# Three gated merges computed by rows instead of by columns, with the sum turned on TensorE

## The chip, the cores and the metric

One Trainium2 chip, one of its cores. The metric is the time of one execution in device microseconds; the time quoted for a kernel is the median of its runs. All arithmetic is 32-bit; matrix operands are split into a high and a low part (`hi`, `lo`, type float32r), so that each product is made of three matmuls: high by high, high by low, low by high.

## What is computed

One block of a streaming encoder on 256 rows of width 2048. Three attention branches (memory, DSA, stick-breaking) each leave 1024 channels per row. The part that the change touches is the merge:

```
gates  = sigmoid(gl + b_gate)                # gl = h @ w_in[:, GL:GL+6144], three blocks of 2048
merged = gates[0] * (o_sb  @ w_branch[0])
       + gates[1] * (o_dsa @ w_branch[1])
       + gates[2] * (o_mem @ w_branch[2])
x = x + merged @ w_out                       # the output projection
```

After it come a norm, an up projection to 11008 columns, a short causal convolution, a gate, and a down projection.

## The kernel before, in words

**Weights.** All weights lie in DRAM as tiles of 128 partitions by up to 1024 values, in the order of use. `w_tiles` (L148) fetches the next one on SP's queue into `raw` (4 buffers), ScalarE copies it to `whi` and VectorE subtracts to get `wlo` (3 buffers each, at high priority), and then the matmuls of that tile follow. A tile of a matrix with 512 columns to a chunk holds 2 row blocks of 128; with 256 columns, 4 row blocks.

**Two ways to multiply.** `proj_cols` (L178) makes the weights stationary: for each row block and each 128 weight columns it runs `whi` against the high and low parts of all 256 rows (512 moving columns) and `wlo` against the high parts (256 moving columns). The result stands with channels on partitions. `proj_rows` (L166) makes the activations stationary: for each row block and each of two row tiles of 128 it runs three matmuls with 512 weight columns moving. The result stands with rows on partitions. In a trace the first reads `pj<-xc,whi` and `pj<-xc,wlo`, the second `pj<-whi,xc` and `pj<-wlo,xc`; `xc` is the normalized input, and `om`, `od`, `osb` (branch outputs), `x2c`, `fc` and `mg` stand in its place elsewhere. A tile is 16 matmuls by columns (8 of 512 and 8 of 256 moving) and 12 by rows (all of 512): 6144 moving columns either way.

**The merge** (L522) runs three times: for the memory branch while the DSA attention is under way, for DSA while stick-breaking attention is under way, and for stick-breaking alone. Each has 8 chunks of 256 columns: 4 tiles of gate weights, an evacuation and tanh on `th`, 2 tiles of branch weights, an evacuation to `pbr`, and the product added into `acc`. The last merge also splits the sum into `mg`, the operand of the output projection. So each merge has 48 weight tiles.

**The order of other work.** After each weight tile, `step()` (L106) runs one due entry of `soon` or one piece of the generator at the head of `later` (attention heads). These pieces put a few matmuls (`s`, `o`) or transposes (`t`) between tiles. The scheduler then fixes each engine's order.

Of the kernel before, what the change touches and what calls it, by code (L numbers as in the profile page):

```python
# [11 lines left out]
F32 = mybir.dt.float32  # L12
# [7 lines left out]
P = 128  # L20
# [15 lines left out]
R1, R2 = -0.6368202810903829, 1.3473041101248473  # 2**12 and 2**22 modulo 2 pi  # L36
# [9 lines left out]
def weight_chunks():  # L46
    """The weight columns in the order of their use: (matrix, row blocks, first column, columns)."""
    for c in range(4):
        yield "kv", KD, c * 512, 512
    for base, n in ((QM, 1024), (KB, 1024), (QB, 1024), (VB, 512), (QI, 256), (QI + 256, 328), (VB + 512, 512)):  # L50
        for c in range(0, n, 512):
            yield "in", KD, base + c, min(512, n - c)
    for br in (2, 1, 0):
        for c in range(0, D, 256):
            yield "in", KD, GL + br * D + c, 256
            yield "b%d" % br, D // 2 // P, c, 256
        if br == 2:
            for base, n in ((KA, 256), (QA, 256), (VA, 512)):
                for c in range(0, 1024, n):
                    yield "in", KD, base + c, n  # L60
    for c in range(4):
        yield "out", KD, c * 512, 512
    for c in range(0, DFF, 256):
        for half in range(2):
            yield "up", KD, half * DFF + c, min(256, DFF - c)
    for c0, n in DOWN:
        yield "down", NFF, c0, n


def weight_tiles():  # L70
    """The chunks cut into tiles of up to 1024 values a partition: (matrix, first row block, row blocks, c0, n)."""
    first = True
    for name, nk, c0, n in weight_chunks():
        j = 0
        while j < nk:
            kn = 1 if first else min(8, 1024 // n, nk - j)
            yield name, j, kn, c0, n
            j += kn
            first = False
# [7 lines left out]
def hybrid_block(ctx: ExitStack, tc: tile.TileContext, x, xT, mem, memT, pos, inv, prm, gqk, wts, out):  # L87
# [14 lines left out]
    # Other work is spread between the weight tiles: each tile is followed by one due entry of `soon`, or else by one  # L102
    # step of the generator at the head of `later`.
# [26 lines left out]
    def heads(n, first, second, third):  # L130
        """The three stages of n heads, two heads under way at a time."""
        first(0)
        yield
        first(1)
        yield
        for h in range(n):
            yield
            second(h)
            yield
            yield  # L140
            if h + 2 < n:
                first(h + 2)
            yield
            third(h)
# [3 lines left out]
    def w_tiles(name, nk, c0, n):  # L148
        """The weight columns c0..c0+n by row block as pairs (hi, lo) of float32r tiles."""
        j = 0  # L150
        while j < nk:
            at, (name_, j_, kn, c0_, n_) = next(tiles)
            assert (name_, j_, c0_, n_) == (name, j, c0, n), (name, j, c0, n)
            raw = wraw.tile([P, 1024], F32, name="raw")
            nc.sync.dma_start(raw[:, :kn * n], wts[at, :, :kn * n])  # L155
            hi = whl.tile([P, 1024], F32R, name="whi")
            lo = whl.tile([P, 1024], F32R, name="wlo")
            with tc.high_priority():
                nc.scalar.activation(hi[:, :kn * n], raw[:, :kn * n], AF.Copy)  # L159
                nc.vector.tensor_sub(lo[:, :kn * n], raw[:, :kn * n], hi[:, :kn * n].bitcast(F32))  # L160
            for k in range(kn):
                yield j + k, hi[:, k * n:(k + 1) * n], lo[:, k * n:(k + 1) * n]
            step()
            j += kn

    def proj_rows(a, name, nk, c0, n):  # L166
        """A PSUM tile [128 rows, 2 row tiles, n] of a.T @ w[:, c0:c0+n]; a is [128, nk, (hi, lo), 256]."""
# [10 lines left out]
    def proj_cols(a, name, nk, c0, n):  # L178
        """A PSUM tile [128 columns, column blocks, (main, rest), 256 rows] of w[:, c0:c0+n].T @ a."""
# [8 lines left out]
    def split(dst, src, scale=1.0):  # L188
        """dst[:, .., (hi, lo), :] of scale * src."""
# [29 lines left out]
    hb = const.tile([P, 48], F32, name="hb")  # L219

    def load_constants():
# [4 lines left out]
        nc.vector.tensor_scalar_mul(hb, prm_sb[:, B_GATE:B_GATE + 48], 0.5)  # L226

    def rsqrt(pool, v, n):
        """1 / sqrt(v) of a small tile [128, n], by Newton's iteration."""
# [9 lines left out]
    def row_squares(ss, rows, src):  # L239
        """The sums of squares of the rows of src [256, 2048], one half of a row tile a step."""  # L240
# [8 lines left out]
    def row_rstd(pool, ss):  # L249
        """[128, 2] of 1 / rms over rows of 2048 with sums of squares ss."""  # L250
# [5 lines left out]
    def bcast_cols(pool, r, name):  # L256
        """[128, 256] with r's entry of row tile tt, row n in column tt * 128 + n of every partition."""
# [10 lines left out]
    with ExitStack() as actx:  # L268
# [54 lines left out]
        def heads256(ps, g0, dst, b0, wait, r=None, r2=None):  # L323
            """RMS norm over 256 channels of two heads in ps (row tiles tt), transposed to dst[:, b0.., rows]."""
# [72 lines left out]
        def weighted_values(o, pt, v_of):  # L397
            """o [128 channels, 256 rows] from pt: keys 0..127 by all rows, then keys 128..255 by rows 128..255."""
# [20 lines left out]
        # the angle modulo 2 pi: angle = 2**22 nh + 2**12 nl + rest, exact but for the last three steps  # L419
# [32 lines left out]
        def rope(dst, src, c1, s2, c2, s1, nh_, half):  # L452
            """dst = (x1 c1 - x2 s2, x2 c2 + x1 s1) for src [128, nh_, 2 * half] in PSUM."""
# [68 lines left out]
        # sigmoid(g) = (1 + tanh(g / 2)) / 2; the half is applied to the sum  # L522
        acc = []

        def merge(br, o, then=None):
            """Adds 2 * sigmoid(gate of branch br) * (o @ its projection) to acc; then(column blocks, sum) if given."""
            first = not acc
            if first:
                acc.extend(h8("acc").rearrange("p (b t) -> p b t", t=T) for _ in range(2))
            for c in range(8):  # L530
                pg = proj_cols(xc, "in", KD, GL + br * D + c * 256, 256)
                th = tg.tile([P, 2, T], F32, name="th")
                nc.scalar.activation(th, pg[:, :, 1, :], AF.Copy)
                nc.vector.tensor_add(th, pg[:, :, 0, :], th)
                for b in range(2):
                    i = br * 16 + c * 2 + b
                    nc.scalar.activation(th[:, b, :], th[:, b, :], AF.Tanh, scale=0.5, bias=hb[:, i:i + 1])
                pb = proj_cols(o, "b%d" % br, 8, c * 256, 256)
                a_ = acc[c // 4][:, (c % 4) * 2:(c % 4) * 2 + 2, :]
                t_ = tg.tile([P, 2, T], F32, name="pbr", bufs=2)  # L540
                nc.scalar.activation(t_, pb[:, :, 1, :], AF.Copy)
                nc.vector.tensor_add(t_, pb[:, :, 0, :], t_)
                if first:
                    nc.vector.scalar_tensor_tensor(a_, th, 1.0, t_, op0=ALU.add, op1=ALU.mult)
                    continue
                nc.vector.scalar_tensor_tensor(t_, th, 1.0, t_, op0=ALU.add, op1=ALU.mult)
                nc.vector.tensor_add(a_, a_, t_)
                if then is not None:
                    then(slice(2 * c, 2 * c + 2), a_)

# [64 lines left out]
        # columns 0..127: rows of tile 0 against keys 0..127; 128..383: rows of tile 1 against all keys  # L615
# [95 lines left out]
        # z is [key, row]: columns 0..255 keys of tile 0 by all rows, 256..383 keys of tile 1 by rows 128..255  # L711
# [37 lines left out]
        merge(0, osb, lambda blocks, a_: split(mg[:, blocks], a_, 0.5))  # L749

# [1 line left out]
        x2c = xp.tile([P, KD, 2, T], F32R, name="x2c", tag="xc")  # L752
        ss = const.tile([P, 2, 4], F32, name="ssx2")
        for c in range(4):
            ps = proj_rows(mg, "out", KD, c * 512, 512)
            x2 = []
            for tt in range(2):
                xr = tg.tile([P, 512], F32, name="xr", tag=("th", "pbr")[tt])
# [69 lines left out]
_ORDER = ["x", "xT", "mem", "memT", "pos", "inv", "prm", "gqk", "wts"]  # L828
# [38 lines left out]
```

## Time and profile before

| what | before |
|---|---|
| median of 3 runs | 1709.14 us (1707.66 to 1709.62) |
| span of the profiled execution | 1706.0 us, so 3.1 us less than the median |
| PE busy | 1695.3 us, 99% of the span |
| VectorE, ScalarE busy | 64%, 52% |
| TensorE clock granted | full in all 40 slices |
| the three merges | 321.91 to 475.03, 609.09 to 759.80, 759.80 to 895.48 us |

Busy time of PE adds pipelined matmuls, so 99% says that it nearly always had one in the pipe, not that it ran at its peak. What counts below is the distance from the start of one matmul to the start of the next. A few per cent of matmul records are missing, so distances are read between rows that stand on either side of a full group.

### The profile page before, as it was taken

How to read it: one execution, taken by the hardware profiler on the slowest of the kernel's cores; microseconds unless marked ns; L12 is line 12 of the kernel's file. 1: busy time of each engine (PE TensorE's matmuls, PEld its weight loads, DVE VectorE, ACT ScalarE, POOL GpSimd, SP SyncE). 2: the span in 40 equal slices, each digit the busy share in tenths (PEclk: the TensorE clock that was granted, in tenths of full speed). 3: DMA queues.
4: the chain of work that ended last, by engine and by line, in shares of the span. 5: the costliest groups of instructions: out<-in, count | busy, mean ns of one | idle time of the engine just before them, and what ended most of it. 6: DMA issues, size and time to landing. Idle time of an engine off the chain costs nothing.

```text
span 1706.0 us, 24002 instructions
## 1 busy us (share of the span) xinstructions
PE 1695.3 (99%) x9202; PEld 1466.1 (86%) x9202; DVE 1088.6 (64%) x1626; ACT 894.8 (52%) x1231; POOL 6.9 (0%) x58
## 2 busy tenths in 40 slices
PE   8999999999999999999999999999999999999999
PEld 6888889888888888888888888888888888888899
DVE  6686865786554455655655577777777777644443
ACT  7555554455544477645554555555555555433432
POOL 0000000000000000000000000000000000000000
PEclk9999999999999999999999999999999999999999
DMA  9755445544455554455556665555555555565663
GB/s 340 263 184 186 148 161 175 185 172 162 162 184 185 190 177 158 166 182 188 186 191 228 223 209 187 194 188 189 193 186 193 190 188 192 188 213 197 219 207 128
DMA packets 96516, 326.60 MB, mean 191 GB/s; under 512 B 10768, under 2 KB 16272, under 8 KB 96400
## 3 DMA queue, kind: packets, MB, share of 16 engines
q1 hardware_dynamic: 95536, 324.00, 55.3%
q8 instruction: 72, 1.18, 0.3%
q10 hardware_dynamic: 864, 1.06, 0.2%
q14 instruction: 44, 0.36, 0.1%
HBM read 320.82 MB, written 4.19 MB: 191 GB/s over the span
## 4 chain that ended last, share of the span: by engine, by line
PE 99%; DMA 0%; DVE 0%; ACT 0%; issue 0%; SPq 0%; DVEq 0%
PE pj L100 95%; PE s L100 2%; PE o L100 1%; DMA mf<-in_memT 0%; PE t L559 0%; PE t L771 0%; PE t L328 0%; PE t L681 0%; DVE xf L372 0%; ACT whi L159 0%; DVE wlo L160 0%; PE t L505 0%; ACT mc L190 0%; DVE xc L192 0%; SPq L155 0%
## 5 line engine op out<-in xcount | busy, mean ns | idle before, releaser
L160 DVE TENSOR_TENSOR wlo<-raw,whi 128x1024 fp32r<-128x1024 f32 (+2 forms) x591 | 719.7, 1218 | 569.7 <-ACT whi L159 568.4
L159 ACT ACTIVATE whi<-raw 128x1024 fp32r<-128x1024 f32 (+2 forms) x591 | 623.0, 1054 | 753.3 <-PE pj L100 579.1
L100 PE MATMUL pj<-x2c,whi 128*128 128x512 f32 x1376 | 477.5, 391 | 0.0
L100 PE MATMUL pj<-x2c,wlo 128*128 128x256 f32 x1376 | 385.5, 280 | 0.0
L100 PE MATMUL pj<-xc,whi 128*128 128x512 f32 x1024 | 366.9, 401 | 0.0
L100 PEld LDWEIGHTS pj<-x2c,whi 128*128 128x128 f32 x1376 | 257.3, 187 | 56.4
L100 PE MATMUL pj<-xc,wlo 128*128 128x256 f32 x1024 | 287.0, 280 | 0.0
L100 PEld LDWEIGHTS pj<-x2c,wlo 128*128 128x128 f32 x1376 | 260.1, 189 | 0.0
L100 PE MATMUL pj<-whi,xc 128*128 128x512 f32 (+2 forms) x768 | 231.7, 379 | 0.5 <-DVE xc L192 0.5
L100 PEld LDWEIGHTS pj<-xc,whi 128*128 128x128 f32 x1024 | 192.4, 188 | 45.6
L100 PE MATMUL pj<-whi,fc 128*128 128x512 f32 (+1 forms) x860 | 221.0, 347 | 0.0
L100 PEld LDWEIGHTS pj<-xc,wlo 128*128 128x128 f32 x1024 | 193.4, 189 | 0.3
L100 PEld LDWEIGHTS pj<-whi,fc 128*128 128x128 f32 x860 | 150.6, 189 | 20.1
L100 PEld LDWEIGHTS pj<-whi,xc 128*128 128x128 f32 x768 | 141.0, 188 | 25.5 <-DVE xc L192 1.0
L100 PE MATMUL pj<-wlo,fc 128*128 128x512 f32 (+1 forms) x430 | 149.1, 347 | 0.0
L100 PE MATMUL pj<-wlo,xc 128*128 128x512 f32 (+2 forms) x384 | 143.6, 374 | 0.0
L100 PEld LDWEIGHTS pj<-wlo,fc 128*128 128x128 f32 x430 | 81.4, 189 | 10.1
L100 PE MATMUL pj<-whi,mc 128*128 128x512 f32 x256 | 81.5, 397 | 5.6 <-ACT whi L159 5.6
L100 PEld LDWEIGHTS pj<-wlo,xc 128*128 128x128 f32 x384 | 72.3, 188 | 11.8
L100 PE MATMUL pj<-whi,mg 128*128 128x512 f32 x256 | 80.6, 392 | 0.0
L100 PEld LDWEIGHTS pj<-whi,mc 128*128 128x128 f32 x256 | 48.7, 190 | 16.0 <-ACT whi L159 6.1
L100 PEld LDWEIGHTS pj<-whi,mg 128*128 128x128 f32 x256 | 48.1, 188 | 9.9
(225 smaller groups left out, 1429.3 us busy)
## 6 DMA issues: line engine op xcount, KB each, us to landing
raw<-in_wts SPq DMA_DIRECT2D x578, 512.0 KB, 3.3
raw<-in_wts SPq DMA_DIRECT2D x5, 492.0 KB, 3.2
nat_rows<-in_mem SPq DMA_DIRECT2D x4, 512.0 KB, 6.5
nat_rows<-in_x SPq DMA_DIRECT2D x4, 512.0 KB, 6.5
xf<-in_xT SPq DMA_DIRECT2D x4, 512.0 KB, 5.6
xr<-in_x SPq DMA_DIRECT2D x8, 256.0 KB, 3.6
x2d<-xr SPq DMA_DIRECT2D x8, 256.0 KB, 4.2
mf<-in_memT SPq DMA_DIRECT2D x3, 512.0 KB, 8.1
```

Source lines behind the costliest of these rows:

```text
L100: nc.tensor.matmul(o, l, r, start=start, stop=stop, skip_group_check=True)
L159: nc.scalar.activation(hi[:, :kn * n], raw[:, :kn * n], AF.Copy)
L160: nc.vector.tensor_sub(lo[:, :kn * n], raw[:, :kn * n], hi[:, :kn * n].bitcast(F32))
```

## The change

The merge uses `proj_rows` with chunks of 512 columns, 4 to a merge (8 gate tiles and 4 branch tiles each, still 48 tiles and the same bytes of weights). The gate bias no longer comes with the tanh instruction as a value per partition; it is fetched from DRAM, the same 512 values to all 128 partitions, once for each row tile, into `th` before the gate result is added. `acc` stands by rows, so in the last merge each finished 512 columns are turned by 8 transposes (4 for each row tile) into a PSUM tile `t`, and split from there into `mg`. They are queued 3 and 4 steps after the end of the chunk.

```diff
-        for c in range(0, D, 256):
-            yield "in", KD, GL + br * D + c, 256
-            yield "b%d" % br, D // 2 // P, c, 256
+        for c in range(0, D, 512):
+            yield "in", KD, GL + br * D + c, 512
+            yield "b%d" % br, D // 2 // P, c, 512
...
-            for c in range(8):
-                pg = proj_cols(xc, "in", KD, GL + br * D + c * 256, 256)
-                th = tg.tile([P, 2, T], F32, name="th")
-                nc.scalar.activation(th, pg[:, :, 1, :], AF.Copy)
-                nc.vector.tensor_add(th, pg[:, :, 0, :], th)
-                for b in range(2):
-                    i = br * 16 + c * 2 + b
-                    nc.scalar.activation(th[:, b, :], th[:, b, :], AF.Tanh, scale=0.5, bias=hb[:, i:i + 1])
-                pb = proj_cols(o, "b%d" % br, 8, c * 256, 256)
-                a_ = acc[c // 4][:, (c % 4) * 2:(c % 4) * 2 + 2, :]
-                t_ = tg.tile([P, 2, T], F32, name="pbr", bufs=2)
-                nc.scalar.activation(t_, pb[:, :, 1, :], AF.Copy)
-                nc.vector.tensor_add(t_, pb[:, :, 0, :], t_)
...
+            for c in range(4):
+                cols = slice(c * 512, (c + 1) * 512)
+                th = tg.tile([P, 2, 512], F32, name="th")
+                for tt in range(2):
+                    nc.sync.dma_start(th[:, tt], bcast_rows(bg[:, br * D + c * 512:br * D + (c + 1) * 512], 512))
+                pg = proj_rows(xc, "in", KD, GL + br * D + c * 512, 512)
+                nc.vector.tensor_add(th, pg, th)
+                nc.scalar.activation(th, th, AF.Tanh, scale=0.5)
+                pb = proj_rows(o, "b%d" % br, 8, c * 512, 512)
+                for tt in range(2):
+                    a_ = acc[tt][:, cols]
+                    if first:
+                        nc.vector.scalar_tensor_tensor(a_, th[:, tt], 1.0, pb[:, tt], op0=ALU.add, op1=ALU.mult)
+                        continue
+                    nc.vector.scalar_tensor_tensor(th[:, tt], th[:, tt], 1.0, pb[:, tt], op0=ALU.add, op1=ALU.mult)
+                    nc.vector.tensor_add(a_, a_, th[:, tt])
                 if then is not None:
-                    then(slice(2 * c, 2 * c + 2), a_)
+                    then(c)
...
-        merge(0, osb, lambda blocks, a_: split(mg[:, blocks], a_, 0.5))
+        def turn_merged(c, tt):
+            pt = pa.tile([P, 512], F32, name="t")
+            for b in range(4):
+                at = (4 * c + b) * P
+                nc.tensor.transpose(pt[:, b * P:(b + 1) * P], acc[tt][:, at:at + P], ident)
+            split(mg[:, 4 * c:4 * c + 4, :, tt * P:(tt + 1) * P], pt.rearrange("p (b t) -> p b t", t=P), 0.5)
+        merge(0, osb, lambda c: [after(3 + tt, partial(turn_merged, c, tt)) for tt in range(2)])
```

In the output projection the two row tiles of the residual, `xr` before, become halves of one tile `xrow`.

On TensorE's queue, the third gate tile of the last merge's second chunk ends, and what follows, before the change at the same weights and after it. Before, columns run on without a break:

```order
L100 MATMUL pj<-xc,whi 128x512
L100 MATMUL pj<-xc,wlo 128x256
L100 MATMUL pj<-xc,whi 128x512
L100 MATMUL pj<-xc,wlo 128x256
L100 MATMUL pj<-xc,whi 128x512
```

After the change the same place reads (`t<-ident,acc` are the new transposes):

```order
L100 MATMUL pj<-whi,xc 128x512
L749 MATMUL t<-ident,acc 128x128 x4
L100 MATMUL pj<-whi,xc 128x512
L100 MATMUL pj<-wlo,xc 128x512
L100 MATMUL pj<-whi,xc 128x512 x2
L100 MATMUL pj<-wlo,xc 128x512
L100 MATMUL pj<-whi,xc 128x512 x2
L100 MATMUL pj<-wlo,xc 128x512
L100 MATMUL pj<-whi,xc 128x512 x2
L100 MATMUL pj<-wlo,xc 128x512
L100 MATMUL pj<-whi,xc 128x512
L749 MATMUL t<-ident,acc 128x128 x4
```

One weight tile (12 matmuls) lies between the two groups of four transposes, and each tile has 12 matmuls where it had 16.

On VectorE's queue, the work on one chunk of 256 columns in the last merge, before:

```order
L534 TENSOR_TENSOR th<-pj,th 128x512
L160 TENSOR_TENSOR wlo<-raw,whi 128x1024 x2
L542 TENSOR_TENSOR pbr<-pj,pbr 128x512
L546 SCALAR_TENSOR_TENSOR pbr<-th,pbr 128x512
L547 TENSOR_TENSOR acc<-acc,pbr 128x512
L160 TENSOR_TENSOR wlo<-raw,whi 128x1024
L194 SCALAR_TENSOR_TENSOR mg<-acc,mg 128x2x256
L160 TENSOR_TENSOR wlo<-raw,whi 128x1024 x3
```

And after the change, on one chunk of 512 columns:

```order
L533 TENSOR_TENSOR th<-pj,th 128x1024
L160 TENSOR_TENSOR wlo<-raw,whi 128x1024 x4
L541 SCALAR_TENSOR_TENSOR th<-th,pj 128x512 x2
L160 TENSOR_TENSOR wlo<-raw,whi 128x1024
L542 TENSOR_TENSOR acc<-acc,th 128x512 x2
L160 TENSOR_TENSOR wlo<-raw,whi 128x1024 x3
L194 SCALAR_TENSOR_TENSOR mg<-t,mg 128x4x128
L160 TENSOR_TENSOR wlo<-raw,whi 128x1024
L194 SCALAR_TENSOR_TENSOR mg<-t,mg 128x4x128
L160 TENSOR_TENSOR wlo<-raw,whi 128x1024 x3
```

The sum into `acc` comes one tile's `wlo` after the products, and the two splits into `mg` come three more tiles later, with one `wlo` between them.

On SP's queue, in the last merge, the bias goes between weight fetches, after the change:

```order
L531 DMA th<-in_bg 128x512 x2
L155 DMA raw<-in_wts 128x1024 x12
L531 DMA th<-in_bg 128x512 x2
L155 DMA raw<-in_wts 128x1024 x12
L531 DMA th<-in_bg 128x512 x2
```

Before, this place was an unbroken run of weight fetches.

## Rows read from the trace of the kernel before

**Rows 1.** The page's part 1: span, and busy time of each engine.

```profile
span 1706.0 us, 24002 instructions
PE 1695.3 (99%) x9202; PEld 1466.1 (86%) x9202; DVE 1088.6 (64%) x1626; ACT 894.8 (52%) x1231; POOL 6.9 (0%) x58
```

**Rows 2.** Waits of PE for another engine: us in total, times, longest.

```profile
PE pj L100 <- ACT whi L159: 5.6, 1, 5.6
```

**Rows 3.** The three merges as stretches: length, busy time of engines, clock, DMA.

```profile
321.91:475.03 153.12, 153.12 (x889) 134.40 (x888) 106.21 (x203) 81.19 (x135) 0.00 (x0) 1.00 0.48 165
609.09:759.80 150.71, 150.71 (x881) 132.63 (x880) 87.99 (x101) 104.99 (x145) 0.00 (x0) 1.00 0.49 168
759.80:895.48 135.68, 135.68 (x770) 117.72 (x769) 83.00 (x87) 69.50 (x87) 0.00 (x0) 1.00 0.54 188
```

**Rows 4.** The chain in time in the first merge: start us, us, what.

```profile
340.55 0.86 PE s L100 x4
...
381.86 0.66 PE s L100 x4
382.51 2.82 PE pj L100 x16
385.33 0.65 PE o L100 x4
```

**Rows 5.** The chain in the second merge, pieces of one stick-breaking head.

```profile
641.34 0.76 PE s L100 x6
...
648.42 0.52 PE s L100 x4
```

**Rows 6.** PE's timeline in the down projection, by rows: start us, us, what.

```profile
1490.37 0.62 PE L100 MATMUL pj<-whi,fc 128*128 128x512 f32 x2
...
1497.17 0.62 PE L100 MATMUL pj<-whi,fc 128*128 128x512 f32 x2
```

**Rows 7.** The chain in a stage by rows with attention steps between tiles.

```profile
211.35 0.44 PE t L505 x4
211.78 2.74 PE pj L100 x12
214.53 0.44 PE t L559 x4
```

**Rows 8.** The chain in the output projection, where a turn waited.

```profile
978.11 0.05 issue
978.16 0.63 PE t L771 x4
```

**Rows 9.** PE's timeline by columns, just after the first merge.

```profile
480.05 0.40 PE L100 MATMUL pj<-xc,whi 128*128 128x512 f32 x1
...
485.70 0.40 PE L100 MATMUL pj<-xc,whi 128*128 128x512 f32 x1
```

**Rows 10.** PE's timeline by columns in the up projection.

```profile
999.84 0.39 PE L100 MATMUL pj<-x2c,whi 128*128 128x512 f32 x1
...
1005.38 0.39 PE L100 MATMUL pj<-x2c,whi 128*128 128x512 f32 x1
```

**Rows 11.** VectorE's timeline just after the last merge's end at 895.48.

```profile
899.29 0.69 DVE L547 TENSOR_TENSOR acc<-acc,pbr 128x512 f32<-128x512 f32 x1
```

**Rows 12.** Groups by form: count, busy us, mean ns of one, idle before.

```profile
L100 PE MATMUL pj<-x2c,whi 128*128 128x512 f32 x1376 | 477.5, 391 | 0.0
L160 DVE TENSOR_TENSOR wlo<-raw,whi 128x1024 fp32r<-128x1024 f32 x578 | 707.9, 1225 | 555.8 <-ACT whi L159 554.5
L190 ACT ACTIVATE mg<-acc 128x512 fp32r<-128x512 f32 x8 | 5.1, 632 | 4.2 <-DVE acc L547 4.2
L559 PE MATMUL t<-ident,nat 128*128 128x128 f32 x44 | 6.7, 272 | 0.0
```

**Rows 13.** DMA of a weight tile (KB, us to landing), and SP's longest wait.

```profile
raw<-in_wts SPq DMA_DIRECT2D x578, 512.0 KB, 3.3
...
SPq L155 <- DVE wlo L160: 1220.6, 511, 5.5
```

More of the change, by code (lines that the diff above doesn't have):

```diff
@@ L86, in hybrid_block @@
 @with_exitstack
-def hybrid_block(ctx: ExitStack, tc: tile.TileContext, x, xT, mem, memT, pos, inv, prm, gqk, wts, out):
+def hybrid_block(ctx: ExitStack, tc: tile.TileContext, x, xT, mem, memT, pos, inv, prm, gqk, bg, wts, out):
     nc = tc.nc
@@ L217, in col @@
         return prm_sb[:, i:i + 1]
-    hb = const.tile([P, 48], F32, name="hb")
     def load_constants():
@@ L225, in load_constants @@
         nc.sync.dma_start(gqk_sb, bcast_rows(gqk, 2 * P))
-        nc.vector.tensor_scalar_mul(hb, prm_sb[:, B_GATE:B_GATE + 48], 0.5)
     def rsqrt(pool, v, n):
@@ L528, in merge @@
             if first:
-                acc.extend(h8("acc").rearrange("p (b t) -> p b t", t=T) for _ in range(2))
-            for c in range(8):
-                pg = proj_cols(xc, "in", KD, GL + br * D + c * 256, 256)
-                th = tg.tile([P, 2, T], F32, name="th")
-                nc.scalar.activation(th, pg[:, :, 1, :], AF.Copy)
-                nc.vector.tensor_add(th, pg[:, :, 0, :], th)
-                for b in range(2):
-                    i = br * 16 + c * 2 + b
-                    nc.scalar.activation(th[:, b, :], th[:, b, :], AF.Tanh, scale=0.5, bias=hb[:, i:i + 1])
-                pb = proj_cols(o, "b%d" % br, 8, c * 256, 256)
-                a_ = acc[c // 4][:, (c % 4) * 2:(c % 4) * 2 + 2, :]
-                t_ = tg.tile([P, 2, T], F32, name="pbr", bufs=2)
-                nc.scalar.activation(t_, pb[:, :, 1, :], AF.Copy)
-                nc.vector.tensor_add(t_, pb[:, :, 0, :], t_)
[L543 to L547, printed above, removed]
@@ new lines, in merge @@
+                acc.extend(h8("acc") for _ in range(2))
+            for c in range(4):
[14 more added lines that the diff above has]
+                    nc.vector.tensor_add(a_, a_, th[:, tt])
@@ L755, in hybrid_block @@
             ps = proj_rows(mg, "out", KD, c * 512, 512)
+            xrow = tg.tile([P, 2, 512], F32, name="xrow", tag="th")
             x2 = []
             for tt in range(2):
-                xr = tg.tile([P, 512], F32, name="xr", tag=("th", "pbr")[tt])
+                xr = xrow[:, tt]
                 nc.sync.dma_start(xr, x[tt * P:(tt + 1) * P, c * 512:(c + 1) * 512])
@@ L825, in hybrid_block @@
                 (nc.sync, nc.scalar)[tt].dma_start(out[tt * P:(tt + 1) * P, c0:c0 + n], xr)
-_ORDER = ["x", "xT", "mem", "memT", "pos", "inv", "prm", "gqk", "wts"]
+_ORDER = ["x", "xT", "mem", "memT", "pos", "inv", "prm", "gqk", "bg", "wts"]
 def kernel(x, mem, positions, attn_norm, mem_norm, w_in, b_gate, dsa_q_norm, dsa_k_norm, mem_q_norm, mem_k_norm,
@@ L856 @@
         "gqk": c(np.concatenate([np.asarray(dsa_q_norm), np.asarray(dsa_k_norm)], axis=0).reshape(1, 2 * P)),
+        "bg": c(np.asarray(b_gate).reshape(1, 3 * D)),
         "wts": wts,
```

## The prediction

> **What bounds the kernel now.** I read the page's busy times first: TensorE has a matmul in the pipe for 1695.3 of 1706.0 us, while VectorE and ScalarE stand at 64% and 52% [rows 1]. Then TensorE's waits: the one long wait for another engine, 5.6 us, is at the start, before any merge [rows 2]. Then the three merges as stretches [rows 3]: 153.12, 150.71 and 135.68 us, together 439.51, with PE busy for the whole length of each, at clock 1.00, and VectorE free for at least 30% of each. So a merge lasts as long as TensorE's queue of matmuls, and the change is worth what it does to the distance from one matmul start to the next, and to the number of starts.
>
> **What a weight tile costs by columns.** The third merge has nothing between its tiles: 135.68 / 48 = 2.827 us a tile, that is 0.353 us for a pair of a 512 and a 256 matmul (8 pairs). In the other two, attention pieces lie between. Their own time in the first merge is 6 index pieces at 0.86 to 0.89 (5.2), 8 scores at 0.66 (5.3), 8 values at 0.65 (5.2) [rows 4] and 8 groups of three transposes at 0.33, three quarters of the 0.44 that four take [rows 7] (2.6): 18.3 us, which leaves 134.8. In the second, 8 scores at 0.76, 8 sums at 0.52 [rows 5] and 8 values at 0.65: 15.4, which leaves 135.3. All tiles together: 134.8 + 135.3 + 135.7 = 405.8 us for 144 tiles, 2.82 each.
>
> **What a tile costs by rows.** The down projection multiplies by rows: 30 matmuls of 512 columns between the two rows shown, 6.80 us, so 0.2267 each and 2.72 for the 12 of a tile [rows 6]. Both ways stream 6144 columns; at 2.4 GHz, the upper of the clock's two levels, that is 2.56 us. The rest is 0.26 us over 16 matmuls, or 0.16 us over 12: about 15 ns each. I take it as a cost of each matmul, so it falls with their number. Next to an attention piece a row tile takes 2.74 [rows 7], which is 0.02 more; there are 30 + 24 = 54 pieces in the first two merges: 1.1 us. The merges by rows: 144 x 2.72 = 391.7, plus 1.1 = 392.8. **First term: 405.8 - 392.8 = 13.0 us gained.** Its bounds: if every tile cost 2.74, 1.8 us less (the 1.1 is then inside it); if no piece cost anything extra, 1.1 more.
>
> **What the turn adds.** 32 transposes in 8 groups of four. From the start of one such group to the next with one row tile between them is 214.53 - 211.35 = 3.18 us [rows 7]; less 2.72 that is 0.46 a group. The dearest group in the trace, which waited for a PSUM tile, took 0.05 + 0.63 = 0.68 [rows 8]. So 3.7 to 5.4 us; I take 0.46 for the first group of each pair and 0.05 more for the second, 3.9. **Second term: 3.9 us lost.**
>
> The second group waits for `t` (one buffer) to be split. ScalarE's half of a split of this size takes 0.63, VectorE's 0.69, a `wlo` 1.23 [rows 11, 12]. If one `wlo` goes first, `t` is free 2.55 us after the first group, and the tile between lasts 2.72: just in time, so a small wait is possible and a long one is not. The first group comes three tiles (8.2 us) after its chunk; before the change, VectorE has the last sum of the last merge done 4.5 us after the merge's end [rows 11], and after it needs two products, one `wlo` and two sums (4 us). The last chunk's turns come after the third and fourth tile of the output projection, and the blocks they fill are read from its seventh tile on, two tiles (5.4 us) later.
>
> **What hides the rest.** ScalarE loses two copies of 512 a chunk of 256, VectorE two additions; neither is on the path, so nothing is gained there. TensorE alternates between two PSUM tiles; by rows it is away for 4 or 8 tiles (11 or 22 us) before it needs one again, against one or two VectorE passes. If that cover were gone, the next chunk's first matmul would wait. The tanh of 1024 values stands on ScalarE before `whi` of later tiles; at most three tiles are split ahead, 8 us of cover. The 24 bias transfers (256 KB, 6.3 MB in all) come on SP's queue, the queue of the weights. From the third chunk on, such a transfer waits until `th` of two chunks earlier is free, and the weights behind it wait too. SP waits for `raw` buffers 511 times [rows 13]: it is early. A tile is issued when the one four before it has been split; its own split starts four tiles after that one's, and a split is ScalarE's pass (taken as no longer than VectorE's) and then VectorE's 1.23 [rows 12], so 4 x 2.82 - 2.46 = 8.8 us after the issue; it lands in 3.3: 5.5 us of slack. A bias transfer is reached about one tile (2.7 us) after the chunk two before it has ended, and `th` is free some 4 us after that end, so SP stands 1 to 2 us and the slack takes it. Priced at nothing; without that cover each lost microsecond counts ten times, once for each chunk from the third on.
>
> **Sum.** 13.0 - 3.9 = 9.1 us. The profiled span 1706.0 becomes 1696.9; the median of the runs lies 3.1 above the span, which I keep: **1700.0 us**.
>
> **A rule that speaks against it.** TensorE spends about 15 ns on a matmul beyond its columns in both ways of multiplying [rows 3, 6]. The Trainium skill, "TensorE: Matmul & The Clock Gate", section "Back-to-back issue gap", gives an isolated gap of N/2.4 + 2.5 ns. By it a column tile would be 2.60 and a row tile 2.59 us, and the change would lose some 2 us. The trace does not agree: it shows 2.83 and 2.72.
>
> Four transposes in a row start and end inside 0.44 us, though each is listed with 272 ns, since they overlap [rows 7, 12]. The same page, section "Part 4: PE-mode transpose", gives about 275 ns for one in a kernel. The listed time agrees; taken as a price it would make the turn 8.8 us and the result 1704.9. The distance, not the length, is what the queue pays.
>
> **Rivals.**
> *The up projection changes step.* Column pairs run at two paces: after the first merge 16 pairs take 5.65 us (0.353 each) [rows 9], in the up projection 16 take 5.54 (0.346) [rows 10], with the same shapes and clock. Which pace a stretch falls into seems to hang on what came just before it. The up projection has 1376 pairs [rows 12] and might come out of the changed output projection at the other pace: 1376 x 0.0069 = 9.5 us lost, 1709.5. For it: both paces occur, and each persists for hundreds of matmuls. Against it: the order of TensorE's rows into the up projection is unchanged. 11%. (The reverse, for the 256 pairs of columns after the first merge, would give 1.8 us: 1698.2; inside my case.)
> *Columns alone set the time.* If the excess belonged to the stage and not to the matmul, row tiles in the merges would cost 2.82 and only the turn would count: 1709.1 + 3.9 = 1713.0, slower. It decides against the change from 2.78 us a tile, where 144 tiles give back no more than the turn. For it: equal columns. Against it: row tiles with the same `xc` and attention between them take 2.74 [rows 7]. The rule above ends near this time. 4%.
> *A new wait at the chunks.* SP, `t` or VectorE's sums are later than reckoned. 0.5 us a chunk is 6 us: 1706; about 1 us a chunk cancels the gain. 8%: mostly between 1703 and 1708. Another 3% for waits that make it slower.
>
> **How the numbers follow.** My case 74%, with a range of its own of 1698 to 1703 from the bounds of the terms. The range 1697 to 1706 takes in most of the new waits and leaves out the changed step. A measurement of this kernel tells 0.2%, 3.4 us, from no change. Faster (under 1705.7): my case and half of the waits, 0.79. Same: the step, the rest of the waits, 0.14. Slower (over 1712.6): 0.07.
>
> **What would show it.** Merges by stretches near 149.5, 146.5 and 133.5 us; 12 matmuls in 2.72 us within them; groups of four transposes at 0.44; PE's waits for VectorE near nothing; the up projection still at 0.346 a pair. I am wrong if row tiles in the merges take 2.8, if PE waits for `t` or for `raw` once a chunk, or if the up projection takes 0.353 a pair.

## The result, and the profile after

| | before | after |
|---|---|---|
| median | 1709.37 us (4 runs) | 1699.80 us (4 runs) |
| span of the profiled execution | 1706.0 us | 1697.8 us |

The ratio is 0.9948, 95% interval 0.9934 to 0.9962: the changed kernel is faster by 0.5%, clear of the noise, by 9.6 us in the medians and 8.2 us in the two profiled spans. A median of 1700.0 had been forecast.

The page's first part, after:

```profile
span 1697.8 us, 22795 instructions
PE 1686.8 (99%) x8658; PEld 1440.5 (85%) x8658; DVE 1071.7 (63%) x1589; ACT 863.5 (51%) x1147; POOL 6.9 (0%) x58
```

TensorE's busy share is 99% as in [rows 1], with 544 matmul records fewer, so the busy share told nothing of the gain. The Trainium skill, "Trainium Kernel Development and Optimization", section "Performance Expectations", calls matmul busy time a bad metric for how close a kernel is to its roofline, because matmuls are pipelined. This pair of traces agrees: 99% before and after.

The stretches of the program after, in order: first merge, the projections between, second merge, third merge, output projection, up projection. Columns as in [rows 3]:

```profile
322.85:472.74 149.89, 149.89 (x697) 124.75 (x696) 101.59 (x192) 70.92 (x108) 0.00 (x0) 1.00 0.55 179
472.74:605.12 132.38, 132.38 (x708) 113.70 (x706) 64.79 (x59) 55.69 (x59) 0.00 (x0) 1.00 0.59 195
605.12:752.74 147.62, 147.62 (x689) 123.61 (x688) 81.53 (x88) 96.10 (x118) 0.00 (x0) 1.00 0.57 182
752.74:886.28 133.54, 133.54 (x601) 110.24 (x600) 76.56 (x74) 58.10 (x58) 0.00 (x0) 1.00 0.63 205
886.28:977.94 91.66, 91.48 (x418) 74.92 (x416) 51.67 (x56) 43.94 (x58) 0.00 (x0) 1.00 0.68 218
977.94:1456.49 478.55, 478.48 (x2764) 421.51 (x2762) 361.54 (x487) 273.31 (x351) 4.37 (x44) 1.00 0.57 192
```

The same stretches before, as far as [rows 3] do not hold them (the projections, the output projection, the up projection):

```profile
475.03:609.09 134.06, 134.06 (x707) 114.52 (x706) 65.28 (x59) 56.08 (x60) 0.00 (x0) 1.00 0.55 188
895.48:986.13 90.65, 90.48 (x411) 74.20 (x409) 50.59 (x54) 44.10 (x58) 0.00 (x0) 1.00 0.67 223
986.13:1464.72 478.59, 478.53 (x2764) 421.56 (x2762) 361.46 (x487) 273.45 (x351) 4.37 (x44) 1.00 0.56 192
```

Subtract line by line. The merges get shorter by 3.23, 3.09 and 2.14 us, and the output projection longer by 1.01 (the last chunk's turns fall there): 7.45 us come from the change's own work. The projections between the first two merges, whose instructions are the same, get shorter by another 1.68. Against that the first merge starts 0.94 later (322.85 for 321.91). The sum is 8.19; the spans differ by 8.2. PE is busy for the whole length of each merge, as before.

The chain in time after, one stick-breaking head of the second merge (to be set beside [rows 5]) and one pair of turns in the third:

```profile
636.90 0.76 PE s L100 x6
637.66 2.79 PE pj L100 x12
640.45 0.65 PE o L100 x4
641.11 2.75 PE pj L100 x12
643.86 0.53 PE s L100 x4
...
827.34 0.44 PE t L749 x4
827.78 2.78 PE pj L100 x12
830.56 0.46 PE t L749 x4
```

Tiles of 12 matmuls stand where tiles of 16 stood. And what PE, or its weight load, waited for in the changed parts (columns as in [rows 2]):

```profile
PE pj L100 <- ACT whi L159: 6.1, 1, 6.1
...
PEld t L749 <- DVE mg L194: 1.0, 4, 0.3
```

The long one is at the program's start, as before. The other is a wait of the weight load: ahead of the second group of each of the four pairs of turns it waits some 0.25 us until `t` is split. The matmuls hardly show it: in the pair above the second group takes 0.46 us where the first takes 0.44, and in none of the four pairs does it delay a transpose by more than 0.06.

### The profile page after: what moved, and what is told of

The parts are those of the page before. It is cut to its first block, busy times and chain, and to the rows that moved or that the text cites. A ratio compares the mean times of both kernels' runs of the same rounds, so it can differ in the third digit from the quotient of the medians.

```text
span 1697.8 us, 22795 instructions
## 1 busy us (share of the span) xinstructions
PE 1686.8 (99%) x8658; PEld 1440.5 (85%) x8658; DVE 1071.7 (63%) x1589; ACT 863.5 (51%) x1147; POOL 6.9 (0%) x58
## 3 DMA queue, kind: packets, MB, share of 16 engines
q10 hardware_dynamic: 864, 1.06, 0.2%
## 4 chain that ended last, share of the span: by engine, by line
PE 99%; DMA 0%; DVE 0%; issue 0%; ACT 0%; SPq 0%; DVEq 0%
PE pj L100 95%; PE s L100 2%; PE o L100 1%; DMA raw<-in_wts 0%; PE t L554 0%; PE t L775 0%; PE t L749 0%; PE t L325 0%; PE t L676 0%; ACT whi L159 0%; DVE xf L369 0%; DVE wlo L160 0%; PE t L502 0%; DVE xc L192 0%; SPq L288 0%
## 5 line engine op out<-in xcount | busy, mean ns | idle before, releaser
L100 PE MATMUL pj<-whi,xc 128*128 128x512 f32 (+2 forms) x1536 | 481.1, 387 | 0.5 <-DVE xc L192 0.5
L100 PEld LDWEIGHTS pj<-whi,xc 128*128 128x128 f32 x1536 | 285.2, 188 | 55.3 <-DVE xc L192 1.0
L100 PE MATMUL pj<-wlo,xc 128*128 128x512 f32 (+2 forms) x768 | 293.3, 382 | 0.0
L100 PEld LDWEIGHTS pj<-wlo,xc 128*128 128x128 f32 x768 | 144.6, 188 | 25.8
L100 PE MATMUL pj<-xc,whi 128*128 128x512 f32 x256 | 88.9, 394 | 0.0
L100 PE MATMUL pj<-xc,wlo 128*128 128x256 f32 x256 | 70.9, 277 | 0.0
L100 PEld LDWEIGHTS pj<-xc,whi 128*128 128x128 f32 x256 | 48.0, 188 | 11.1
L100 PE MATMUL pj<-wlo,mc 128*128 128x512 f32 x128 | 51.2, 400 | 0.4 <-DVE wlo L160 0.4
```

Source lines behind the costliest of these rows:

```text
L100: nc.tensor.matmul(o, l, r, start=start, stop=stop, skip_group_check=True)
```

## The experiments

The theory: a matmul costs its columns plus a fixed 13 to 15 ns, so fewer and wider matmuls are faster; the turn costs its own length; all else hides. Rivals: the arrangement (weights moving) makes the gain; columns alone count; the bias transfers or the turns hold something up. All experiments start from the changed kernel where nothing else is said.

**More matmuls for the same columns.** `proj_rows` takes `cuts`, the number of pieces of each of its three matmuls; the merges use (2, 2, 2) in one kernel and (1, 1, 2) in the other.

```diff
-    def proj_rows(a, name, nk, c0, n):
+    def proj_rows(a, name, nk, c0, n, cuts=(1, 1, 1)):
...
-                mm(d, lh, hi, kt == 0, False)
-                mm(d, lh, lo, False, False)
-                mm(d, ll, hi, False, kt == nk - 1)
+                for i, (l_, r_) in enumerate(((lh, hi), (lh, lo), (ll, hi))):
+                    w_ = n // cuts[i]
+                    for q in range(cuts[i]):
+                        mm(d[:, q * w_:(q + 1) * w_], l_, r_[:, q * w_:(q + 1) * w_], i == 0 and kt == 0,
+                           i == 2 and kt == nk - 1)
```

> The changed kernel with every matmul of the merges cut into two of 256 columns: 24 a tile in place of 12, the same columns, operands and results. If each matmul costs its columns plus some 15 ns, a tile takes 24 x 0.120 = 2.88 us (0.120 is the distance of such matmuls in the last 512 columns of the down projection) and the merges 144 x 0.16 = 23 us more: about 1723 us, slower than before the change though it multiplies by rows. If what counts is that weights move and activations stand (the arrangement), or the columns alone, the merges stay within 2 us of the changed kernel: about 1700 us.

Unlike what the expectation says, the results are not the same: with (2, 2, 2) the matmul that opens an accumulation is cut too, each half opens one of its own in the same PSUM bank, and the merged sums change; that the opening is the reason is not shown. The columns and the number of matmuls are as described. Measured: 1722.94 us, ratio 1.0079 (1.0065 to 1.0093), 23.1 more than the changed kernel. In the two traces the three merges are 6.41, 7.04 and 7.30 us longer, 20.8 together. Another 1.7 lie in the projections after the first merge, whose column pairs ran at a slower pace here (134.08 us for 132.38; more on this pace below):

```profile
478.13:612.21 134.08, 134.08 (x707) 114.52 (x706) 64.79 (x59) 55.63 (x59) 0.00 (x0) 1.00 0.58 192
```

> The changed kernel with one of three matmuls of the merges (low by high) cut into two of 256 columns: by rows, but with the tile's mix of by columns, 8 of 512 and 8 of 256. If the number of matmuls makes the time, a tile takes 8 x 0.2267 + 8 x 0.120 = 2.77 us, or 2.83 if it falls into the slower of the two paces that column pairs show: 7 to 15 us more than the changed kernel, 1707 to 1715, so most or all of the gain is gone. If the arrangement makes the time, 2.72 us a tile and about 1700 us.

Measured: 1707.44 us, ratio 0.9992 (0.9982 to 1.0001): no different from before the change, at the low end of the 1707 to 1715 expected if the number of matmuls makes the time. Eleven bare tiles between two turns of the third merge, in the chain of each kernel; first the changed kernel (12 matmuls a tile):

```profile
797.38 29.96 PE pj L100 x132
```

With 16 a tile:

```profile
802.88 30.66 PE pj L100 x176
```

With 24 a tile:

```profile
813.98 31.68 PE pj L100 x264
```

A tile takes 2.724, 2.787 and 2.880 us. Less the 2.56 us of its 6144 columns, that is 13.6, 14.2 and 13.3 ns for each matmul. The number makes the time. The arrangement alone gives nothing in the end: 16 by rows take 2.79 us a tile where 16 by columns took 2.82, some 4.4 us over the 144 tiles, and the turns cost about as much (4.04, below). The Trainium skill, "TensorE: Matmul & The Clock Gate", section "Back-to-back issue gap", has 2.5 ns beyond the columns for an isolated matmul; an estimate by it would make 24 a tile 0.03 us a tile dearer, 4 us in all. The trace does not agree: the merges took 20.8 us more.

**No turn.**

```diff
-            for b in range(4):
-                at = (4 * c + b) * P
-                nc.tensor.transpose(pt[:, b * P:(b + 1) * P], acc[tt][:, at:at + P], ident)
-            split(mg[:, 4 * c:4 * c + 4, :, tt * P:(tt + 1) * P], pt.rearrange("p (b t) -> p b t", t=P), 0.5)
+            split(mg[:, 4 * c:4 * c + 4, :, tt * P:(tt + 1) * P],
+                  acc[tt][:, c * 512:(c + 1) * 512].rearrange("p (b t) -> p b t", t=P), 0.5)
```

> The changed kernel without the 32 transposes: the split into mg reads the sum as it stands, by rows, so the block that the output projection gets is not turned. If the turn costs TensorE its own length and nothing waits for it, 8 groups at 0.46 to 0.5 us come off: 1695.8 us. If the turn also holds up what follows (the wait for t, late sums), more than 5 us come off; if its transposes were hidden in the queue, nothing.

Measured: 1697.15 us, ratio 0.9931 (0.9918 to 0.9943), 2.65 less than the changed kernel. The stretches of the third merge and of the output projection in its trace:

```profile
754.09:884.65 130.56, 130.56 (x578) 108.11 (x576) 76.56 (x74) 58.31 (x58) 0.00 (x0) 1.00 0.67 210
884.65:975.25 90.60, 90.47 (x410) 74.20 (x408) 51.68 (x56) 44.02 (x58) 0.00 (x0) 1.00 0.69 221
```

They are 2.98 and 1.06 us shorter than after the change: the turn costs 4.04 us, 0.50 a group, and nothing behind it. The whole kernel gained 1.4 us less than that, since the first merge here began that much later (324.20 for 322.85), behind code that is the same.

**No bias.**

```diff
-                for tt in range(2):
-                    nc.sync.dma_start(th[:, tt], bcast_rows(bg[:, br * D + c * 512:br * D + (c + 1) * 512], 512))
                 pg = proj_rows(xc, "in", KD, GL + br * D + c * 512, 512)
-                nc.vector.tensor_add(th, pg, th)
+                nc.vector.tensor_copy(th, pg)
```

> The changed kernel without the 24 bias transfers: the gate result is copied out of PSUM and the bias is left out. If the transfers hide behind the slack of the weight tiles, as priced, the time stays within 1 us of the changed kernel, 1699 to 1700. If they hold up the weights (at the chunks, or where four of them come early, among the input's transfers), the merges get shorter by up to 0.5 us a chunk, or the first merge starts up to 1 us earlier: 1694 to 1699.

Measured: 1700.63 us, ratio 0.9949 (0.9936 to 0.9961). The three merges, in its trace:

```profile
323.98:473.87 149.89, 149.89 (x697) 124.77 (x696) 101.59 (x192) 70.92 (x108) 0.00 (x0) 1.00 0.51 169
...
606.25:753.87 147.62, 147.62 (x689) 123.60 (x688) 81.53 (x88) 96.11 (x118) 0.00 (x0) 1.00 0.52 171
753.87:887.41 133.54, 133.54 (x601) 110.26 (x600) 76.56 (x74) 58.10 (x58) 0.00 (x0) 1.00 0.58 193
```

Each merge has the same length to 0.01 us with and without 6.3 MB of transfers: they are hidden. The first merge starts at 323.98 without them and at 322.85 with them, so these traces give no sign that the later start after the change is theirs either. That start lies between 321.8 and 324.2 in the profiles named so far, in no order that an edit explains; why it varies was not tried.

**The pace of column pairs.** One to four idle transposes, whose result is not read, ahead of the columns after the first merge and again after the last turn at the up projection (k is 1 to 4; the same lines stand at both places). In TensorE's queue the second ones came some 11 us into the up projection, behind its first 28 or so pairs.

```diff
+        pk = pa.tile([P, 512], F32, name="t")
+        for q in range(k):
+            nc.tensor.transpose(pk[:, q * P:(q + 1) * P], ident, ident)
```

> The changed kernel with one idle transpose (its result is not read) put into TensorE's queue just before the columns after the first merge, and one just after the last turn ahead of the up projection. If the pace of column pairs hangs on what came just before, one or both stretches change to the other pace: the 256 pairs after the first merge from 0.3467 to 0.3533 (1.7 us more), the 1376 of the up projection likewise (9.2 us more, about 1709 in all). If the pace belongs to the stage (its data, its neighbours on the other engines), both stay at 0.3467 and the time rises by 0.2 us at most.

> As with one idle transpose, with two in each place. If what came before sets the pace, some of one, two, three and four give 0.3533 in one of the stretches and others 0.3467; if the stage sets it, none does.

> As with one idle transpose, with three in each place. Three transposes ahead of columns went with the slower pace in the first merge of the kernel before; if that is the rule, the stretches run at 0.3533: 1.7 and 9.2 us more, some 1710 us. If the stage sets the pace, 0.3467 and 1700 us.

> As with one idle transpose, with four in each place. Some of the four kernels at the other pace in some stretch if what came before sets it; all of them at 0.3467 and within 0.5 us of the changed kernel if the stage does.

| idle transposes | pair after the first merge, us | pair in the up projection, us | median us | ratio |
|---|---|---|---|---|
| 0 (the changed kernel) | 0.3467 | 0.3467 | 1699.80 | 0.9948 (0.9934 to 0.9962) |
| 1 | 0.3467 | 0.3467 | 1700.20 | 0.9945 (0.9922 to 0.9967) |
| 2 | 0.3467 | 0.3533 | 1710.11 | 1.0007 (0.9996 to 1.0018) |
| 3 | 0.3533 | 0.3533 | 1711.48 | 1.0007 (0.9992 to 1.0021) |
| 4 | 0.3533 | 0.3533 | 1711.58 | 1.0011 (0.9998 to 1.0024) |

The pace is the mean distance of pair starts in the one profiled execution of each kernel. PE's timeline of the up projection with two transposes, sixteen pairs apart, to be set beside [rows 10]:

```profile
999.75 0.40 PE L100 MATMUL pj<-x2c,whi 128*128 128x512 f32 x1
...
1005.40 0.40 PE L100 MATMUL pj<-x2c,whi 128*128 128x512 f32 x1
```

And with one:

```profile
999.93 0.39 PE L100 MATMUL pj<-x2c,whi 128*128 128x512 f32 x1
...
1005.48 0.39 PE L100 MATMUL pj<-x2c,whi 128*128 128x512 f32 x1
```

5.65 against 5.55 us. The whole up projection with two transposes:

```profile
978.02:1465.80 487.78, 487.65 (x2765) 422.75 (x2764) 362.22 (x487) 273.20 (x351) 4.36 (x44) 1.00 0.56 188
```

That is 9.2 us more than the 478.55 after the change. The two transposes are worth 0.26 us themselves; the step of pace costs the other 9.0, over pairs that are the same, in the same order. (The medians differ by 10.3; the last 1.1 us are not assigned.) So the stage alone does not set the pace: transposes put before the pairs changed it. Each kernel has them at both places, so that the nearer ones did it is likely and not shown apart, nor is it shown whether it is the transposes themselves or the shift in time that they bring. One of the eight runs with three transposes took 1703.14 us, and one with four 1704.26, some 8 and 7 under their medians. That is near the price of the step, so the same program may take either pace, rarely; no trace of these runs shows it.

**The same in the kernel before**, ahead of the columns after the first merge and ahead of the third merge, with one, two and three.

> The kernel before the change with one idle transpose ahead of the columns after the first merge and one ahead of the third merge, both of which ran at 0.3533 a pair. If what came before sets the pace, one or both may drop to 0.3467: 1.7 us less for the first, 2.6 us less for the third merge (384 pairs), 1705 to 1709 us. If the pace belongs to the kernel by columns at these places, both stay and the time is 1709.5.

> As the kernel before the change with one idle transpose, with two in each place: 0.3467 in one or both stretches and down to 1705 us, or no change at all.

> As the kernel before the change with one idle transpose, with three in each place: 0.3467 in one or both stretches and down to 1705 us, or no change at all. At least one of the three kernels differs from the kernel before if what came before sets the pace.

Measured: 1709.22, 1709.36 and 1708.41 us; ratios 0.9999 (0.9989 to 1.0009), 1.0009 (0.9996 to 1.0022), 0.9992 (0.9982 to 1.0002). One of the eight runs with two took 1718.88, 9.5 over its median; no trace shows why. Only three transposes, and only ahead of the first of the two places, moved the pace. PE's timeline there, to be set beside [rows 9]:

```profile
479.80 0.40 PE L100 MATMUL pj<-xc,whi 128*128 128x512 f32 x1
...
485.35 0.40 PE L100 MATMUL pj<-xc,whi 128*128 128x512 f32 x1
```

The third merge stayed at 0.3533 in all three. So what brings a stretch to one pace or the other is not the number of transposes alone: three led to the faster pace here, and to the slower one at the same place of the changed kernel.

**Wider matmuls elsewhere.** The down projection's last 512 columns in one chunk.

```diff
-DOWN = ((0, 512), (512, 512), (1024, 512), (1536, 256), (1792, 256))
+DOWN = ((0, 512), (512, 512), (1024, 512), (1536, 512))
```

> The changed kernel with the last 512 columns of the down projection as one chunk of 512 in place of two of 256: 258 matmuls of 512 in place of 516 of 256, the same columns. If the number of matmuls makes the time, 516 x 0.120 - 258 x 0.2267 = 3.4 us come off TensorE; the last result is twice as wide, so VectorE's additions and the transfer behind the last matmul take up to 1.3 us longer: 1697 to 1698 us. If columns alone count, only the longer end is left: 1700 to 1701.

Measured: 1697.49 us, ratio 0.9931 (0.9917 to 0.9944), the shortest of all complete kernels. The down projection after the change, to its last matmul, was 1456.49 to 1694.00, 237.51 us; here:

```profile
1457.84:1692.00 234.16, 234.12 (x1034) 193.57 (x1032) 110.16 (x102) 90.97 (x90) 0.00 (x0) 1.00 0.59 196
```

3.35 us less for 258 matmuls fewer, which is 13.0 ns each. Behind the last matmul the profile has 5.1 us in place of 3.8, the longer end that was expected. The median is 2.3 us less than the changed kernel's, but the two intervals overlap, so that the whole kernel is faster rests on this stretch and on the medians.

## Why the prediction was right, and where its terms were off

**The bound.** Right: PE stays busy through each merge, and the merges came out at 149.89, 147.62 and 133.54 us for a forecast of 149.5, 146.5 and 133.5.

**First term, forecast 13.0, measured 11.4.** With the same pieces and the turns taken out, the tiles take 131.6, 132.2 and 130.6 us, together 394.4 for a forecast of 392.8. The bare tile was right (130.56 / 48 = 2.72, in the kernel without the turn). What was too small is the 0.02 us beside an attention piece: tiles there take 2.75 to 2.79 in the chain above, and the 54 pieces cost 2.7 us in place of 1.1.

**Its reason was half of it.** The prediction put the whole difference between a column tile and a row tile to the number of matmuls. Its "about 15 ns each" covers 16 ns by columns (0.26 us over 16) and 13 by rows (0.16 over 12), and that gap is the second cause. At the faster pace a column tile is 8 x 0.3467 = 2.77 us, or 13.3 ns a matmul beyond its columns, the same fixed cost as by rows; at the slower pace it is 2.83. Both stood in the merges before: in the first, a tile near the start took

```profile
341.41 2.78 PE pj L100 x16
```

and later ones 2.82 [rows 4]. All 144 column tiles at 2.77 would have been 399.4 us, not 405.8. So up to 6.4 of the 11.4 us came from the slower pace, which streams of 512 alone, as by rows, did not show, and some 5 from the number, of which the turn takes 4. Had the old merges run at the faster pace throughout, the change would have brought about 1 us by this reckoning; that is an estimate, since no run brought a whole merge by columns to the faster pace.

**Second term, forecast 3.9, measured 4.04.** Right, with a small wait for `t` at each second group, where it was looked for (0.25 us of the weight load, 0.02 to 0.06 in the starts of the transposes, for 0.05 forecast).

**What was priced at nothing.** Right for the bias transfers (equal to 0.01 us without them) and for the evacuations.

**The rivals.** The up projection kept its pace, and the step was priced rightly: 9.5 us forecast, 9.0 where two idle transposes brought it about. The reverse step in the 256 pairs after the first merge, named in brackets, did happen: 1.68 us. The change itself was worth 7.5 us in the spans, for 9.1 forecast; this step and a start of the merges 0.94 us later make it 8.2. The medians differ by 9.6 because the profiled span before lay 3.4 us under its median (1709.37) and the one after 2.0. The prediction kept 3.1 for that distance: its span came out 0.9 us too short and its distance 1.1 too long. That the forecast met the median to 0.2 us is thus luck in part: the change's own gain was 1.6 us smaller than forecast, the pace after the first merge gave 1.7, the later start took 0.9, and the shorter distance to the median gave 1.1. Columns alone and new waits at the chunks are out.

## What to carry to other kernels

Where TensorE is full, count matmuls as well as columns: here each costs some 13 ns beyond its columns, so 512 wide beats 256 wide by 6% for the same columns. Read it from the distance of starts in a bare stretch, not from busy time. And compare the distance of identical rows between two traces before explaining a difference: a stretch that nobody touched can change pace, and here the pace may have been worth as much as the number of matmuls.

## What had not been expected of the hardware

Pairs of a 512 and a 256 matmul settle at one of two mean distances, 0.3467 or 0.3533 us, and keep it for up to 1347 pairs. The clock was 1.00 in both. With two idle transposes, 0.26 us of work, nearly the whole up projection ran at the other pace, 9 us longer. Streams of equal matmuls showed one distance each (0.2267 at 512 columns, 0.1200 at 256). Their sum is the faster pace, 0.3467, so it is the slower one that adds something, 6.7 ns a pair. What in the queue decides between the two paces is open: neither the number of transposes nor the place alone does.
